# Six of eleven down-projection blocks by seven products in feed-forwards 2 to 4, with part of the weight sums made ahead and kept in DRAM

## The chip, the core and the metric

The kernel runs on one core of a Trainium2 chip. The metric is the device time of one execution in microseconds (us). The engines of the core are TensorE (PE: matmuls; its weight loads are listed as PEld), VectorE (DVE), ScalarE (ACT), GpSimd (POOL) and SyncE (SP), which issues the transfers; 16 DMA engines carry them. MiB is 1,048,576 bytes, GB/s counts in 10^9 bytes.

## The reference

The kernel computes a small streaming encoder in float32: 256 tokens of width 1024, two layers. Each layer is a feed-forward, a mixer, and a second feed-forward, each added to the residual `h`; the mixer is a convolution module in layer 0 and latent attention in layer 1. A normalisation ends the whole. So there are four feed-forwards, which are numbered here 1 to 4 in order of time, with the convolution between 1 and 2 and the attention between 3 and 4.

```python
D_MODEL, SEQ, D_FF = 1024, 256, 2816

def rmsnorm(x, g):
    return x * lax.rsqrt(jnp.mean(x * x, axis=-1, keepdims=True) + 1e-6) * g

def swiglu_ffn(h, w1, w3, w2):
    return (jax.nn.silu(h @ w1) * (h @ w3)) @ w2

for i in range(2):
    h = h + 0.5 * swiglu_ffn(rmsnorm(h, ffn_norm1[i]), ffn1_w1[i], ffn1_w3[i], ffn1_w2[i])
    m = rmsnorm(h, mix_norm[i])
    h = h + (conv_module(m, ...) if i == 0 else mla(m, positions, ...))
    h = h + 0.5 * swiglu_ffn(rmsnorm(h, ffn_norm2[i]), ffn2_w1[i], ffn2_w3[i], ffn2_w2[i])
return rmsnorm(h, final_norm)
```

## The kernel before

**Numbers.** A float32 product is made of three matmuls of a faster format: each operand is split into a high part, which is the operand rounded by a cast, and a low part, which is the rest. `mm3` issues high x low, high x high and low x high into one bank of the accumulator. For weights the split is made in the kernel: ACT casts the raw block (`hi`, L171 and L193), DVE subtracts (`lo`, L175 and L194).

**Weights.** All weights come as blocks of 128 x 2048 float32 (1 MiB). The list `blocks` holds them in order of use. A block is loaded by SP into one of four buffers `raw`, split into one of four pairs `hi`, `lo`, and used. `load` issues one block's load and split; `load_ahead` and `weights` say how far ahead of the matmuls in the code this is written. What a load really waits for is the `raw` buffer of four blocks earlier, which is free when that block's subtraction is done; a subtraction waits for the pair that the matmuls of four blocks earlier read. Subtractions and casts are written `behind` the last urgent instructions of their engine.

**A feed-forward.** It has two stages. The *gate stage* works through 22 weight blocks in six groups (`c` from 0 to 5; the last is half as wide). After a group's matmuls ACT makes the sigmoid-weighted gate, DVE multiplies, and `turn` brings the result into the transposed layout that the next matmuls need: a 32 x 32 transpose on DVE, four DMAs into DRAM (`gd`, L649), and one DMA back (`gb`, L651), all on SP; then ACT and DVE split it into `Gh` and `Gl`. The *down-projection* (class `Rows`, tiles `o`) works through 11 blocks, each of two 128-row slices of w2, for two token tiles of 128 and two column halves of 512: 2 x 2 x 2 = 8 products, 24 matmuls. The last two blocks (9 and 10) are done in `finish`, one output tile after the other, so that the residual additions (L587) and the next stage's normalisation and transposes (`early`, tiles `tp`) can begin with the first tokens.

**Seven products.** A block is a product of two 2 x 2 matrices of tiles (token tiles by row slices, row slices by column halves). For the blocks in `FAST` this is done with seven products instead of eight (21 matmuls), after Strassen and Winograd. It needs four sums of the weight's quarters and sums of the activations. The weight's sums are made by `load_fast` in a second `raw` buffer, `sums`: two by one POOL instruction (L185), one each by two DVE additions (L186, L187). So a fast block takes two `raw` buffers and two pairs, and both `raw` and `sums` are split, 3.5 times 1024 columns in all. The activations' sums are made by `combine` (POOL, L632) from the turned gates. Of the seven products three go straight into output banks and four into banks `p`, which are kept over all fast blocks and combined by `fold` (L572 to L580: ACT, DVE, and POOL, which adds to `h`) behind the last fast block. In every feed-forward `FAST` is (0, 2, 4, 6, 8): fast and plain blocks alternate, and the fold is behind block 8.

**Order.** Each engine works through its instructions in a fixed order. It is set when the kernel is built by a planner that goes through the code's instructions by priority with estimated times; `urgent` raises a function's priority, `order` fixes one instruction's place behind another's on the same engine without a wait. SP issues all loads and the turns' DMAs from one queue.

**The end.** After feed-forward 4 the class `Final` normalises. Its gain row `gf` and its output pieces `hg` have buffers of their own in the feed-forward's pool.

Of the kernel before, what the change touches and what calls it, by code (L numbers as in the profile page):

```python
# [45 lines left out]
FAST = (0, 2, 4, 6, 8)  # L46
# [41 lines left out]
def trunk(ctx: ExitStack, tc: tile.TileContext, x, xt, pos, invf, gains, gfin, wdw,  # L88
# [27 lines left out]
    conv_block = {}  # L116
    for i in range(2):
        for w13, w2 in ((f1w13, f1w2), (f2w13, f2w2)):

            for cc_ in range(5):  # L120
                for m in range(2):
                    blocks += [w13[i, m, 2 * cc_ + a_] for a_ in range(2)]
            blocks += [w13[i, a_, 10] for a_ in range(2)]
            blocks += [("fast", w2[i, a_]) if a_ in FAST else w2[i, a_] for a_ in range(NF // 2)]
# [28 lines left out]
    def load(src, pieces=1):  # L153
        if isinstance(src, tuple) and src[0] == "fast":
            return load_fast(src[1])
        if isinstance(src, tuple):
# [21 lines left out]
    def load_fast(src):  # L178
# [7 lines left out]
        behind(nc.vector.tensor_add(t[:, 2, :], t[:, 0, :], v[:, 3, :]))  # L186
        behind(nc.vector.tensor_add(t[:, 3, :], t[:, 2, :], v[:, 2, :]))  # L187
# [23 lines left out]
    def slots(b):  # L211
        return 2 if isinstance(blocks[b], tuple) and blocks[b][0] == "fast" else 1
# [267 lines left out]
    class Final:  # L480
        def __init__(self, act):
            self.act = act
            self.gf = act.tile([P, D], F32, tag="gf", name="gf")
            nc.sync.dma_start(self.gf, gfin.partition_broadcast(P))

            self.e = [None] * NT
            self.n = [0] * NT
            self.y = {}

        def piece(self, tb, c):  # L490

            n = c.stop - c.start
            t = self.act.tile([P, 512], F32, tag="hg", name=uid("hg"), bufs=4)
# [26 lines left out]
    class Rows:  # L520
        def __init__(self, zh, zl, nk, last=False, sh=None, sl=None):
            self.zh, self.zl, self.nk, self.last = zh, zl, nk, last
            self.sh, self.sl = sh, sl
            self.o = {(tb, d): bank("A", "o") for tb in range(NT) for d in range(2)}
            self.begun = set()
            self.early = max(i for i in range(nk // 2 - 2) if sh is None or i not in FAST)

# [20 lines left out]
        def fast(self, i):  # L548

            n = FAST.index(i)  # L550
# [6 lines left out]
            for o, key, (ah, al), (hi, lo), q in (  # L557
                    (self.p[0], "p1", z(f, 0), raw, 0), (self.o[0, 0], (0, 0), z(f + 1, 0), raw, 2),
                    (self.o[0, 1], (0, 1), s(2), raw, 3), (self.p[2], "p5", z(f, 1), sums, 0),
                    (self.p[3], "q7", s(1), sums, 1), (self.p[1], "q6", s(0), sums, 2),  # L560
                    (self.o[1, 0], (1, 0), z(f + 1, 1), sums, 3)):
                c = slice(q * 512, q * 512 + 512)
                mm3(o, ah, al, hi[:, c], lo[:, c], self.begin(key), isinstance(key, str) and i == FAST[-1])
            if i == FAST[-1]:
                self.fold()
# [46 lines left out]
    def ffn(X, make_next, beside=lambda: None):  # L612
        with tc.tile_pool(name=uid("ffn"), bufs=1) as act:
            return ffn_in(act, X, make_next, beside)

    def ffn_in(act, X, make_next, beside):
        Gh = act.tile([P, NF, S], F32R, tag="Gh", name=uid("Gh"))
        Gl = act.tile([P, NF, S], F32R, tag="Gl", name=uid("Gl"))
        Sh = act.tile([P, 3 * len(FAST), P], F32R, tag="Sh", name=uid("Sh"))
        Sl = act.tile([P, 3 * len(FAST), P], F32R, tag="Sl", name=uid("Sl"))  # L620
# [6 lines left out]
        def combine(i, b0, b1):  # L627

            n = FAST.index(i)
            sx = act.tile([P, 4, P], F32, tag="sx", name=uid("sx"))  # L630
            v = sx.rearrange("p s (i q) -> p s i q", q=32)
            sub = lambda o, a, b: nc.gpsimd.tensor_tensor(o, a, b, op=ALU.subtract)  # L632
            sub(v[:, 3], b1[:, 0], b1[:, 1])
            sub(v[:, 0], b0[:, 0], v[:, 3])
            sub(v[:, 1], b1[:, 0], b0[:, 0])
            sub(v[:, 2], b0[:, 1], v[:, 0])
            split(Sh[:, 3 * n:3 * n + 3, :], Sl[:, 3 * n:3 * n + 3, :], sx[:, :3, :])
            split(Gh[:, 2 * i, tbs(1)], Gl[:, 2 * i, tbs(1)], sx[:, 3, :])

        def turn(c, tb, w, g):  # L640
# [10 lines left out]
            nc.sync.dma_start(b[:, :w], d)  # L651
# [3 lines left out]
            t0 = 0  # L655
            if tb == 1 and 2 * c in FAST:
                t0 = 1
                combine(2 * c, first[c], bv)
            f = slice(4 * c + t0, 4 * c + n)
            gh, gl = (G_[:, f, tbs(tb)].rearrange("p t (i q) -> p t i q", q=32) for G_ in (Gh, Gl))  # L660
            split(gh, gl, bv[:, t0:])
# [49 lines left out]
        o = Rows(Gh, Gl, NF, make_next is Final, Sh, Sl)  # L711
        for i in range(NF // 2 - 2):
            (o.fast if i in FAST else o.block)(i)
# [663 lines left out]
```

## Time and profile before

| | |
|---|---|
| median of three runs | 925.11 us (922.67 to 925.63) |
| profiled execution | 923.62 us, of which span 921.8 us |
| granted TensorE clock | 0.999 |
| PE busy | 909.6 us, 99% of the span |
| DVE, ACT, POOL busy | 74%, 59%, 25% |
| moved by DMA | 191.58 MB, 208 GB/s on average |
| feed-forward 2 in the trace | gates 286 to 404 us, down-projection 404 to 461 us |
| feed-forward 3 in the trace | gates to 583 us, down-projection 583 to 639 us |
| feed-forward 4 in the trace | gates to 858 us, down-projection 858 to 915 us |

A row of the trace in order of time gives the start and the duration in us, the engine, the line of the kernel, the operation, the tile written and the tiles read, the shape, and the number of like instructions that are merged in it; in brackets stands the time for which the engine had been idle, and what ended it. SPq is SP's queue, and its rows are the issue of a transfer, not the transfer. A row of waits gives the waiting engine, tile and line, what it waited for, the total, the count and the longest. A row of a stretch gives its two ends, the length, then the busy time of PE, PEld, DVE, ACT and POOL with the number of instructions, the granted clock, the DMA engines' share and GB/s.

### The profile page before, as it was taken

The numbers are of one execution on the slowest core, as the hardware profiler recorded it, in microseconds if no ns is written. First come the engines' busy times: TensorE is split into PE (matmuls) and PEld (weight loads), VectorE is DVE, ScalarE is ACT, GpSimd is POOL, SyncE is SP. The second block draws the span as 40 slices with busy tenths as digits, with TensorE's granted clock in tenths as the row PEclk, the third lists the DMA queues.
The fourth block names the chain that finished last, engine by engine and source line by source line (L and its number), as shares of the span: only waits on it lengthen the run. The fifth ranks groups of instructions, "written<-read, shape, count | busy, mean of one in ns | idle before, by whom it ended". The sixth has DMA issues, their size and how long they took to land.

```text
span 921.8 us, 12383 instructions
## 1 busy us (share of the span) xinstructions
PE 909.6 (99%) x4293; PEld 755.5 (82%) x4293; DVE 680.9 (74%) x1052; ACT 539.7 (59%) x940; POOL 226.4 (25%) x337
## 2 busy tenths in 40 slices
PE   9999999999999999999999999999999999999997
PEld 6888888898958888888888888888998788888886
DVE  5776877689977666777976667978667476667876
ACT  6964556568877455455474544655666475444643
POOL 1101232379941100232300003224200000013223
PEclk9999999999999999999999999999999999999999
DMA  9976656653307676556756775656441557774651
GB/s 342 350 276 226 203 180 222 240 183 138 138 22 283 244 255 240 189 161 228 299 205 238 252 244 153 228 209 214 183 183 60 186 202 251 246 239 150 219 183 47
DMA packets 60399, 191.58 MB, mean 208 GB/s; under 512 B 11184, under 2 KB 33328, under 8 KB 40752
## 3 DMA queue, kind: packets, MB, share of 16 engines
q1 hardware_dynamic: 59760, 190.09, 58.9%
q8 instruction: 34, 0.56, 0.2%
q10 hardware_dynamic: 576, 0.69, 0.2%
q14 instruction: 29, 0.24, 0.1%
HBM read 178.17 MB, written 12.58 MB: 207 GB/s over the span
## 4 chain that ended last, share of the span: by engine, by line
PE 72%; DVE 8%; DMA 8%; ACT 4%; issue 3%; POOL 3%; SPq 1%; POOLq 0%; ACTq 0%; DVEq 0%
PE u L288 15%; PE u L287 15%; PE u L284 15%; DVE lo L175 5%; PE o L284 3%; PE o L287 3%; PE o L288 3%; PE gate L738 3%; DMA raw<-in_f2w 3%; DMA raw<-in_f1w 3%; PE u L738 3%; POOL sums L185 3%; PE o L978 2%; ACT hi L171 1%; DVE lo L194 1%
## 5 line engine op out<-in xcount | busy, mean ns | idle before, releaser
L175 DVE TENSOR_TENSOR lo<-raw,hi 128x1024 fp32r<-128x1024 f32 (+1 forms) x246 | 296.3, 1240 | 74.4 <-ACT hi L171 74.1
L171 ACT CAST hi<-raw 128x1024 fp32r<-128x1024 f32 (+1 forms) x250 | 247.9, 1046 | 147.7 <-PE u L288 107.9
L288 PE MATMUL u<-hi,Xl 128*128 128x512 f32 x688 | 267.8, 390 | 0.7 <-DVE Xl L345 0.7
L284 PE MATMUL u<-lo,Xh 128*128 128x512 f32 x688 | 268.1, 390 | 0.1
L287 PE MATMUL u<-hi,Xh 128*128 128x512 f32 x688 | 267.7, 389 | 0.0
L288 PEld LDWEIGHTS u<-hi,Xl 128*128 128x128 f32 x688 | 129.1, 188 | 28.2 <-DVE Xl L345 1.6
L284 PEld LDWEIGHTS u<-lo,Xh 128*128 128x128 f32 x688 | 129.2, 188 | 27.3 <-DVE lo L175 0.5
L287 PEld LDWEIGHTS u<-hi,Xh 128*128 128x128 f32 x688 | 129.2, 188 | 26.6
L185 POOL TENSOR_TENSOR sums<-raw 128x1024 f32<-128x1024 f32 x20 | 54.2, 2710 | 162.4 <-DMA raw<-in_f2w 52.7
L284 PE MATMUL o<-lo,Gh 128*128 128x512 f32 (+1 forms) x236 | 91.5, 388 | 0.7 <-DVE lo L175 0.7
L287 PE MATMUL o<-hi,Gh 128*128 128x512 f32 (+1 forms) x236 | 91.0, 386 | 0.0
L288 PE MATMUL o<-hi,Gl 128*128 128x512 f32 (+1 forms) x236 | 91.0, 386 | 0.0
L632 POOL TENSOR_TENSOR sx<-gb 128x128 f32<-128x128 f32 x20 | 10.2, 509 | 316.7 <-DMA gb<-gd 316.7
L624 ACT CAST Gh<-gb 128x512 fp32r<-128x512 f32 (+2 forms) x48 | 25.8, 539 | 63.6 <-DMA gb<-gd 63.5
L193 ACT CAST hi<-sums 128x1024 fp32r<-128x1024 f32 x40 | 41.2, 1052 | 30.7 <-PE u L288 14.7
L786 DVE SCALAR_TENSOR_TENSOR acc<-V,dw,acc 128x128 f32<-128x128 f32 (+1 forms) x174 | 57.8, 411 | 0.0
L625 DVE TENSOR_TENSOR Gl<-gb,Gh 128x512 fp32r<-128x512 f32 (+2 forms) x48 | 33.2, 705 | 31.2 <-ACT Gh L624 31.1
L194 DVE TENSOR_TENSOR lo<-sums,hi 128x1024 fp32r<-128x1024 f32 x40 | 56.1, 1432 | 0.0
L284 PEld LDWEIGHTS o<-lo,Gh 128*128 128x128 f32 x236 | 44.3, 188 | 11.0 <-DVE lo L175 2.3
L288 PEld LDWEIGHTS o<-hi,Gl 128*128 128x128 f32 x236 | 44.3, 188 | 8.9
L287 PEld LDWEIGHTS o<-hi,Gh 128*128 128x128 f32 x236 | 44.3, 188 | 8.8
L814 ACT ACTIVATE prod<-V,dw 128x128 f32<-128x128 f32 (+1 forms) x129 | 48.0, 418 | 2.8 <-POOL Y L815 1.4
(247 smaller groups left out, 1325.7 us busy)
## 6 DMA issues: line engine op xcount, KB each, us to landing
raw<-in_f2w SPq DMA_DIRECT2D x66, 1024.0 KB, 4.8
raw<-in_f1w SPq DMA_DIRECT2D x64, 1024.0 KB, 5.0
raw<-in_cw SPq DMA_DIRECT2D x12, 1024.0 KB, 5.2
gd<-gt SPq DMA_DIRECT2D x160, 64.0 KB, 2.7
gb<-gd SPq DMA_DIRECT2D x40, 256.0 KB, 3.4
raw<-in_wo SPq DMA_DIRECT2D x4, 1024.0 KB, 4.8
raw<-in_wuq SPq DMA_DIRECT2D x3, 1024.0 KB, 4.8
raw<-in_f1w SPq DMA_DIRECT2D x8, 256.0 KB, 6.2
```

Of the source, the lines that this page charges most:

```text
L171: behind(nc.scalar.copy(hi[:, c], raw[:, c]))
L175: behind(nc.vector.tensor_sub(lo[:, c], raw[:, c], hi[:, c].bitcast(F32)))
L185: behind(nc.gpsimd.tensor_tensor(t[:, 0:2, :], v[:, 0:4:3, :], v[:, 1:2, :].to_broadcast([P, 2, 512]), op=ALU.add))
L193: behind(nc.scalar.copy(hi[:, c0:c1], x[:, c0:c1]))
L194: behind(nc.vector.tensor_sub(lo[:, c0:c1], x[:, c0:c1], hi[:, c0:c1].bitcast(F32)))
L284: mm = nc.tensor.matmul(o, ah, bl, start=start, stop=False)
L287: nc.tensor.matmul(o, ah, bh, start=False, stop=False)
L288: return nc.tensor.matmul(o, al, bh, start=False, stop=stop)
L625: nc.vector.tensor_sub(dl, x, dh.bitcast(F32))
L738: mm = nc.tensor.matmul(u[:, t], w[:, c], X.x[:, k, t], start=(k == 0), stop=(k == KT - 1))
L786: ins = nc.vector.scalar_tensor_tensor(out if j == j1 - 1 else y, v, w, y, op0=ALU.mult, op1=ALU.add)
L814: prod = nc.scalar.activation(p, v, AF.Copy, scale=w)
```

## The change

In feed-forward 1 the fast blocks remain 0, 2, 4, 6 and 8. In feed-forwards 2 to 4 they are 0, 2, 4, 5, 6 and 7. Blocks 0 and 2 make their sums as before. The sums of blocks 4 to 7 are made during the gate stage of the same feed-forward by `sum_ahead`: the block is loaded into a `raw` buffer (a *job*, behind the loads of the gate blocks 4, 7, 10 and 13), DVE makes the four sums in place by four additions, and SP stores them to DRAM. Later `load_summed` loads three quarters of the raw block and all four sums, as two and one transfers, behind the last turn in SP's order.

```diff
-FAST = (0, 2, 4, 6, 8)
+FAST = ((0, 2, 4, 6, 8), (0, 2, 4, 5, 6, 7))
+AHEAD = {4: 4, 5: 7, 6: 10, 7: 13}
...
+            first = len(blocks) == 22
+            for a_ in range(NF // 2):
+                w = w2[i, a_]
+                if not first and a_ in AHEAD:
+                    jobs[len(blocks) - a_ - 22 + AHEAD[a_]] = (a_, w)
+                    w = ("summed", w, a_)
+                elif a_ in FAST[0 if first else 1]:
+                    w = ("fast", w)
+                blocks.append(w)
...
-        behind(nc.vector.tensor_add(t[:, 2, :], t[:, 0, :], v[:, 3, :]))
-        behind(nc.vector.tensor_add(t[:, 3, :], t[:, 2, :], v[:, 2, :]))
+        behind(nc.vector.tensor_add(t[:, 3, :], t[:, 0, :], v[:, 3, :]))
+        behind(nc.vector.tensor_add(t[:, 2, :], t[:, 3, :], v[:, 2, :]))
+        return split_fast(raw, sums)
+
+    def sum_ahead(a, src):
+        raw = rawp.tile([P, HB], F32, tag="raw", name=uid("job"))
+        nc.sync.dma_start(raw, src)
+        v = raw.rearrange("p (b n) -> p b n", n=512)
+        for to, x, y in ((0, 0, 1), (1, 1, 3), (3, 0, 3), (2, 3, 2)):
+            behind(nc.vector.tensor_add(v[:, to, :], v[:, x, :], v[:, y, :]))
+        summed[a] = dram.tile([P, HB], F32, tag=f"summed{a}", name=uid("summed"))
+        nc.sync.dma_start(summed[a], raw)
+
+    def load_summed(src, a):
+        raw = rawp.tile([P, HB], F32, tag="raw", name=uid("raw"))
+        sums = rawp.tile([P, HB], F32, tag="raw", name=uid("sums"))
+        for c in (slice(0, 512), slice(1024, HB)):
+            order(nc.sync.dma_start(raw[:, c], src[:, c]), last_turned[-1].ins)
+        order(nc.sync.dma_start(sums, summed[a]), last_turned[-1].ins)
+        return split_fast(raw, sums)
...
     def load_to(last):
         while len(loaded) < last:
-            loaded.append(load(blocks[len(loaded)], PIECES))
+            b = len(loaded)
+            loaded.append(load(blocks[b], PIECES))
+            if b in jobs:
+                sum_ahead(*jobs[b])
```

`split_fast` is the loop of casts and subtractions that stood at the end of `load_fast`. `last_turned` collects each turn's DMA back from DRAM.

With two fast blocks in one gate group (4 and 5, 6 and 7), `combine` makes both blocks' activation sums by the same four POOL instructions at twice the width, and the splits are wider too. The fold stands behind block 7, the last fast one; block 8 is plain. In `Final`, `gf` uses the buffer of the low part of the normalised activations, `Xl`, and the pieces use the turn's buffers:

```diff
-            self.gf = act.tile([P, D], F32, tag="gf", name="gf")
+            self.gf = xp.tile([P, KT, S], F32, tag="Xl", name="gf").rearrange("p k t -> p (k t)")[:, :D]
...
-            t = self.act.tile([P, 512], F32, tag="hg", name=uid("hg"), bufs=4)
+            tag, bufs = (("gb", 3), ("gt", 2))[len(self.y.get(tb, ())) % 2]
+            t = self.act.tile([P, 512], F32, tag=tag, name=uid("hg"), bufs=bufs)
...
             b = act.tile([P, 512], F32, tag="gb", name=uid("gb"), bufs=3)
-            nc.sync.dma_start(b[:, :w], d)
+            last_turned.append(nc.sync.dma_start(b[:, :w], d))
...
-            if tb == 1 and 2 * c in FAST:
-                t0 = 1
-                combine(2 * c, first[c], bv)
+            if tb == 1 and 2 * c in fasts:
+                count = 2 if 2 * c + 1 in fasts else 1
+                own = slice(1, n, count)
+                combine(c, count, first[c], bv)
```

In feed-forward 4 the output tile of the second tokens and the right columns, into which only plain blocks are accumulated, is added to `h` after block 8 instead of after block 7.

More of the change, by code (lines that the diff above doesn't have):

```diff
@@ L116, in trunk @@
     conv_block = {}
+    jobs = {}
     for i in range(2):
@@ L211, in slots @@
     def slots(b):
-        return 2 if isinstance(blocks[b], tuple) and blocks[b][0] == "fast" else 1
+        return 2 if isinstance(blocks[b], tuple) and blocks[b][0] in ("fast", "summed") else 1
     def load_ahead(ahead=W_BUFS - 2):
@@ L710, in ffn_in @@
                 turn(c, tb, w, g)
-        o = Rows(Gh, Gl, NF, make_next is Final, Sh, Sl)
+        o = Rows(Gh, Gl, NF, make_next is Final, Sh, Sl, fasts)
         for i in range(NF // 2 - 2):
-            (o.fast if i in FAST else o.block)(i)
+            (o.fast if i in fasts else o.block)(i)
             beside()
```

59 lines of the change are left out of this document (32 added, 27 removed).

## The prediction

> **What bounds the kernel now.** I read the page first, for the engine that is busy throughout, then the waits of TensorE, then its order of time in one feed-forward.
>
> ```profile
> PE 909.6 (99%) x4293; PEld 755.5 (82%) x4293; DVE 680.9 (74%) x1052; ACT 539.7 (59%) x940; POOL 226.4 (25%) x337
> ...
> PE 72%; DVE 8%; DMA 8%; ACT 4%; issue 3%; POOL 3%; SPq 1%; POOLq 0%; ACTq 0%; DVEq 0%
> ```
>
> TensorE (PE) is busy 99% of 921.8 us. Its waits:
>
> ```profile
> PE u L288 <- DVE Xl L345: 0.7, 2, 0.4
> PE o L284 <- DVE lo L175: 0.7, 2, 0.4
> ...
> PE a L288 <- DVE Xl L345: 0.3, 1, 0.3
> ```
>
> All that TensorE waits in the change's neighbourhood is there (total, times, longest). So time falls only with matmuls that go or with these small waits, and rises only where the change makes TensorE wait. The price of a matmul, from feed-forward 2 (the first matmul of down-projection blocks 0 and 8):
>
> ```profile
> 404.13 0.39 PE L284 MATMUL p<-lo,Gh 128*128 128x512 f32 x1
> ...
> 444.93 0.39 PE L284 MATMUL p<-lo,Gh 128*128 128x512 f32 x1
> ```
>
> Between them lie blocks 0 to 7, four of seven products (7 x 3 = 21 matmuls) and four plain (2 x 2 x 2 x 3 = 24): 180 matmuls in 40.80 us, 0.2267 us each, without a gap. (0.39 is one matmul's own time; they overlap.) A plain block is 5.44 us, a fast one 4.76.
>
> **The change part by part.**
>
> *Products.* Six fast blocks in place of five in feed-forwards 2, 3 and 4: 3 x 3 = 9 matmuls less, 9 x 0.2267 = **-2.04 us**. Nothing hides matmuls on a gapless TensorE, so this much is certain.
>
> *The sums of blocks 4 to 7.* Before, a fast block's sums were made just ahead of its use: one POOL instruction and two DVE adds, which stand in DVE's fixed order before other blocks' subtractions. In feed-forward 4 this cost TensorE something:
>
> ```profile
> 888.23 2.40 POOL L185 TENSOR_TENSOR sums<-raw 128x1024 f32<-128x1024 f32 x1 [8.13 <-DMA raw<-in_f2w]
> 890.67 0.69 DVE L186 TENSOR_TENSOR sums<-sums,raw 128x512 f32<-128x512 f32 x1 [4.09 <-POOL sums L185]
> 893.01 1.22 DVE L175 TENSOR_TENSOR lo<-raw,hi 128x1024 fp32r<-128x1024 f32 x1
> 893.66 0.39 PE L288 MATMUL o<-hi,Gl 128*128 128x512 f32 x1
> 894.28 0.50 PE L284 MATMUL o<-lo,Gh 128*128 128x512 f32 x1 [0.23 <-DVE lo L175]
> 894.62 0.40 PE L287 MATMUL o<-hi,Gh 128*128 128x512 f32 x1
> ```
>
> DVE sat 4.09 us behind POOL with block 8's sums, so block 7's second subtraction ended at 894.23. From 893.66 to 894.62 are 0.96 us where two matmuls take 0.45. Sums now remain only for blocks 0 and 2, long before block 7: **-0.5 us**. Late next there is the cast of a plain block, which waits for a weight slot and not for sums.
>
> *The jobs beside the gates.* Four a feed-forward: 1 MiB read, four DVE adds in place, 1 MiB written. The adds are like the 0.69 above, 0.6 apart: 16 x 0.6 = 9.6 us of DVE.
>
> ```profile
> 286.00:404.10 118.10, 118.10 (x522) 97.78 (x521) 83.39 (x97) 61.04 (x81) 16.61 (x20) 1.00 0.65 222
> 448.00:452.00 4.00, 4.00 (x20) 3.30 (x19) 3.41 (x4) 3.43 (x4) 1.73 (x1) 1.00 1.01 428
> ...
> 365.06 0.33 SPq L168 DMA_DIRECT2D raw<-in_f2w  x1
> ```
>
> The first row is the gate stage (busy us of PE, PEld, DVE, ACT, POOL, then clock, DMA share, GB/s): DVE goes from 83.4 to 93 of 118 us. With the DMA engines full they move 428 GB/s (next row), that is 2.5 us a MiB, so 8 MiB is 20 us and the share goes from 0.65 to about 0.82. Both fit. What waits: the store stands in SP's queue until its adds are done, and behind it stand the next gate loads and the turns' small DMAs. The last row says what those loads can bear: it is the last gate block's load, issued at 365.06 for matmuls that begin one block (5.44) before 404.13, at 398.7, so 33 us ahead. A job holds one of four raw buffers for a time, which takes at most one block, 5.4 us, of that lead. DVE queues subtractions behind adds that wait for their load; a weight slot comes free three blocks (16 us) before its next use, and a subtraction pair is 2.3. I take 0. Without that cover the adds would cost 9.6 us a feed-forward (upper bound); below nothing I see no reason for.
>
> A 1 MiB store does not occur in the trace. From below it is the load's 2.5 us, from above the 4.8 of a whole load from issue to landing; it ends some 60 us before it is read, so either is free.
>
> *The run of blocks 4 to 7.* Each needs 0.75 MiB of raw columns and 1 MiB of sums: 1.75 x 2.5 = 4.4 us of DMA, 3.5 subtractions and casts of 1024 columns.
>
> ```profile
> 430.43 2.35 DVE L194 TENSOR_TENSOR lo<-sums,hi 128x1024 fp32r<-128x1024 f32 x2
> 429.76 2.00 ACT L171 CAST hi<-raw 128x1024 fp32r<-128x1024 f32 x2
> 412.41 0.34 SPq L651 DMA_DIRECT2D gb<-gd  x1
> raw<-in_f2w SPq DMA_DIRECT2D x66, 1024.0 KB, 4.8
> ```
>
> DVE needs 3.5 x 1.17 = 4.1 us, ACT 3.5, TensorE 4.76: TensorE stays the slowest, DMA close behind. The new order puts these loads behind the last turn, which was issued at 412.41, 8.3 us into the stage. I follow feed-forward 2 (block starts from 404.13: block 4 at 424.5, then 429.3, 434.0, 438.8, block 8 at 443.6), four raw buffers and four weight slots used in turn. Block 4's raw half is issued about 412.7 and lands within 4.8, 417.5; its sums land 2.5 later, 420.0; block 5's halves follow by 424, and block 4 has both subtractions done by 422.5, its start being 424.5. From there each half's subtraction waits for the slot of the half two blocks earlier: block 6's sums get theirs at 429.3, are done by 431.6, needed at 436.1 (after three products); block 7's: 434.0, 436.3, 440.9. **4.5 us are left at each**, and its load is issued at 426.8 and lands about 431.7, 2.3 before the slot. I take 0. The other end stands below as a rival.
>
> The Trainium skill, "DMA: Bandwidth & Descriptors", section "Where 436 GB/s comes from", sets the HBM limit of a core at about 358 GB/s; the row above, with 428, contradicts it here. By that limit a block's 1.84 MB would take 5.1 us (an estimate by that page), 0.4 more than TensorE, 1.5 over the four; it speaks against the change, and is why the supply rival gets more than a token chance.
>
> *Sums of activations for two blocks at once, the swapped order of two sums, the final norm's buffers.* POOL subtracts 256 columns instead of 128 twice, due over 20 us later; same instructions in another order; the gain row is now loaded into a buffer whose last reader is the gate matmul at 858, against a first use at 909. One DVE add of the last stage comes a block later. Zero each; without cover some 0.7 us (one DVE instruction).
>
> *The fold behind block 7.* Its four POOL and five other instructions now start about 440.9 instead of 447.04 (2.1 us after the last fast block's start, as before), while the finishing groups start at 449.0, not 449.7.
>
> ```profile
> 447.04 0.57 ACT L572 COPY fold<-p 128x512 f32<-128x512 f32 x1
> 457.78 0.68 DVE L579 TENSOR_TENSOR fold<-p,fold 128x512 f32<-128x512 f32 x1
> 458.38 1.87 DVE L587 TENSOR_TENSOR h<-o,h 128x512 f32<-128x512 f32 x3
> 458.60 1.29 POOL L580 TENSOR_TENSOR h<-h,fold 128x512 f32<-128x512 f32 x1 [1.83 <-DVE fold L579]
> 460.57 1.47 PE L327 MATMUL tp<-ident,h 128*128 128x128 f32 x12
> 462.11 0.40 PE L287 MATMUL u<-hi,Xh 128*128 128x512 f32 x1
> 462.79 0.50 PE L288 MATMUL u<-hi,Xl 128*128 128x512 f32 x1 [0.28 <-DVE Xl L345]
> 639.08 1.47 PE L327 MATMUL tp<-ident,h 128*128 128x128 f32 x12
> ...
> 641.29 0.50 PE L288 MATMUL a<-hi,Xl 128*128 128x512 f32 x1 [0.28 <-DVE Xl L345]
> 183.38 1.95 PE L453 MATMUL tp<-dR,h 128*128 128x128 f32 x16
> 185.08 0.47 PE L284 MATMUL o<-lo,Gh 128*128 128x512 f32 x1
> ```
>
> Before, the fold ran into the next stage's subtractions; three additions to h came in one lump at 458.38, so all twelve transposes stand behind the last product (460.57), and the next matmuls wait for casts and subtractions: from 462.11 to 462.79 0.45 us too much, with its neighbours about 0.6. The joint at 639.08 is its twin. In feed-forward 1, where the additions were not late, transposes stand inside the stream (183.38, products again at 185.08). Now the fold, 12.9 us long in feed-forward 2 (447.04 to 459.89), ends at 453.8 at worst, while the second group ends at 449.0 + 5.44 = 454.4. So the first rows' eight transposes can go in among the last two groups and those waits go: 2 x 0.6 less some 0.1 for the change of shape: **-1.1 us**, between 0 (the planner leaves them behind) and -1.3. I take -1.1, as feed-forward 1 shows it. Feed-forward 4 ends in no such joint.
>
> **The sum.** -2.04 - 0.5 - 1.1 = -3.6 us. The profiled execution took 923.62 (span 921.8 and 1.8 around it), so 920.0 by its own time; it lies 1.5 below the median of the three runs, 925.11 (they spread over 3.0 us). Against the median: 921.5, a ratio of 0.996. About 0.3%, 2.8 us, is what a measurement of this kernel can tell from no change, so the forecast stands just beyond it.
>
> **The rivals.**
>
> *A, the forecast*, 921.5 (920.0 to 923.0): chance 0.50.
>
> *B, the joints stay as they are*: the planner fixes each engine's order when the kernel is built and may leave the transposes behind the last product. For it: the twins do so now. Against: the additions' lateness goes. -2.04 - 0.5: 922.6. Chance 0.25.
>
> *C, DVE stands at a job's add for a load that is late*, as it did for 4.09 us above, and subtractions behind it come late. One such stand cost TensorE 0.5 there; beside the gates the slots are 16 us ahead, which speaks against. With 12 jobs, at 0.3 each: +3.6, so 925.1. Chance 0.13.
>
> *S, the run starves, and it is slower.* Place: blocks 4 to 7, loads behind the last turn, 7 MiB (7.34 MB) in 19.0 us of products. They have 19.0 + 2.3 + 4.5 = 25.8 us before TensorE waits: nothing is lost down to 284 GB/s. Slower by 2.8 than before needs (2.8 + 3.6) / 3 = 2.1 us a feed-forward, so 263 GB/s or less. The mean of this stage before was:
>
> ```profile
> 404.10:461.00 56.90, 56.90 (x254) 47.11 (x253) 48.23 (x52) 32.63 (x42) 17.93 (x13) 1.00 0.69 244
> ```
>
> At 244 the run takes 30.1, 4.3 too long, 12.9 over three: 925.1 - 3.6 + 12.9 = 934.4. For it: that mean, and SP issues in order, so one blocked issue holds all behind it. Against: 244 was all that was asked, and 428 came when more was. Chance 0.12.
>
> **How the numbers follow.** Faster by over 0.3%: 0.85 of A and 0.3 of B, 0.50. Slower: S and a little of C, 0.14. The rest, 0.36, within. The range 919.5 to 927.0 holds A, B and C with the runs' spread, and leaves out most of S and a little below.
>
> **What would show it.** Right: four fast blocks in a row at 4.76 us each with no wait for a subtraction; no wait at block 7 of feed-forward 4; no POOL sums beyond blocks 0 and 2; transposes inside the last products of feed-forwards 2 and 3, and the 0.45 us gone. Wrong: waits for DVE subtractions in blocks 5 to 8 (S, with loads landing after their slot is free), waits in the gates (C), or twelve transposes still behind the last product (B).

## The result, and the profile after

The changed kernel took **930.72 us** (median of six runs, 929.86 to 933.54) against 924.8 for the kernel before (six runs as well): a ratio of **1.0075**, 95% interval 1.0057 to 1.0093. It is slower; the prediction, 921.5 in a range of 919.5 to 927.0, had the wrong sign. Its profiled execution took 929.86 us with a span of 928.1, 6.25 more than before.

The engines' line of the page and the waits of TensorE (waiting engine, tile and line, what it waited for; total, times, longest) show where it went:

```profile
PE 909.0 (98%) x4284; PEld 753.3 (81%) x4284; DVE 706.3 (76%) x1082; ACT 544.8 (59%) x940; POOL 210.6 (23%) x316
```

```profile
PE p L326 <- DVE lo L233: 2.6, 3, 1.2
PE tp L369 <- DVE h L630: 2.3, 2, 1.2
PE o L326 <- DVE lo L189: 1.7, 3, 1.2
```

TensorE has the nine matmuls less that were forecast (4293 to 4284), and 6.6 us of waits in these three rows, where the three rows quoted of before have 1.7 together. By stretches, from a down-projection's first product to the next stage's first matmul (the last one to the end of the span):

| stretch | before | after | difference |
|---|---|---|---|
| down-projection of feed-forward 2 | 57.67 | 60.44 | +2.77 |
| of feed-forward 3 | 57.67 | 61.21 | +3.54 |
| of feed-forward 4, with the end | 63.98 | 66.06 | +2.08 |
| up to feed-forward 2's down-projection | 404.13 | 403.02 | -1.10 |
| between the down-projections | 120.83 and 217.55 | 120.30 and 217.04 | -0.53 and -0.51 |

Everything that was lost was lost in the three down-projections, each of which has 0.68 us of products less. There are four places. Each size below is the excess of the step between two neighbouring matmuls over the usual 0.227.

*In the run of blocks 4 to 7:* 3.05 us, at 435.37 (0.39), 617.79 (1.39) and 900.03 (1.27). The trace in order of time, in feed-forward 3, for block 6's sums:

```profile
607.13 0.33 SPq L223 DMA_DIRECT2D sums<-summed  x1
615.43 1.99 ACT L232 CAST hi<-sums 128x1024 fp32r<-128x1024 f32 x2 [3.15 <-DMA sums<-summed]
616.51 2.36 DVE L233 TENSOR_TENSOR lo<-sums,hi 128x1024 fp32r<-128x1024 f32 x2 [2.52 <-ACT hi L232]
617.79 0.50 PE L326 MATMUL p<-lo,Gh 128*128 128x512 f32 x1 [1.23 <-DVE lo L233]
```

The transfer was issued at 607.13 and landed at 615.33, 8.2 us later. ACT and DVE stand idle for it (3.15 and 2.52), and TensorE for the subtraction: the data are late, no engine is.

*Behind the run:* 2.20 us at 452.49, 634.01 and 911.52, where `finish` waits for a subtraction of blocks 9 and 10.

*At the joints:* 2.64 us. The trace at feed-forward 2's end:

```profile
454.61 4.58 DVE L189 TENSOR_TENSOR lo<-raw,hi 128x1024 fp32r<-128x1024 f32 x3
459.12 1.87 DVE L630 TENSOR_TENSOR h<-o,h 128x512 f32<-128x512 f32 x3
459.85 0.65 PE L369 MATMUL tp<-ident,h 128*128 128x128 f32 x4 [1.17 <-DVE h L630]
461.51 0.60 PE L369 MATMUL tp<-ident,h 128*128 128x128 f32 x4
463.11 0.60 PE L369 MATMUL tp<-ident,h 128*128 128x128 f32 x4
```

The transposes did move in among the last products, four at a time, as forecast. But the first of them waits for the additions to `h`, which stand in DVE's order behind the subtractions of the next stage's first two blocks.

*At the end:* from the last matmul's start (919.85; before 914.89) to the end of the span 8.22 us, before 6.94.

```profile
910.33 2.28 POOL L621 TENSOR_TENSOR h<-h,fold 128x512 f32<-128x512 f32 x1
912.58 1.30 POOL L623 TENSOR_TENSOR h<-h,fold 128x512 f32<-128x512 f32 x1
913.90 1.29 DVE L630 TENSOR_TENSOR h<-o,h 128x512 f32<-128x512 f32 x2 [1.84 <-POOL h L623]
```

Before, the same first addition waited for TensorE:

```profile
908.26 0.69 DVE L587 TENSOR_TENSOR h<-o,h 128x512 f32<-128x512 f32 x1 [2.08 <-PE o L288]
```

The fold is stretched out between subtractions, POOL's part of it ends at 913.88, and DVE's closing chain starts 5.95 us ahead of the last matmul instead of 6.63.

With 0.51 at 588.35, where the third down-projection waits for the last gate, these waits make 9.68 us; the products (-2.04), the wait of before at 894.28 (-0.51), the old joint waits (-1.04) and the earlier part (-1.10) take off 4.7. That leaves 5.0 of the 6.25; of the other 1.3, 0.8 is the matmul right behind seven of these waits, which each time starts another 0.11 us late, and the rest lies in smaller pieces, which I did not trace.

The page's list of transfers (KB each, median us from issue to landing) shows the change in the latencies; before they were 4.8 for `raw<-in_f2w`, 3.4 for `gb<-gd` and 2.7 for `gd<-gt`:

```profile
raw<-in_f2w SPq DMA_DIRECT2D x58, 1024.0 KB, 7.5
summed<-job SPq DMA_DIRECT2D x12, 1024.0 KB, 8.1
sums<-summed SPq DMA_DIRECT2D x12, 1024.0 KB, 7.6
gd<-gt SPq DMA_DIRECT2D x160, 64.0 KB, 3.9
gb<-gd SPq DMA_DIRECT2D x40, 256.0 KB, 6.2
```

The gate stage of feed-forward 2 took no longer (118.10, as before), with the jobs in it:

```profile
284.90:403.00 118.10, 118.10 (x522) 97.78 (x521) 91.51 (x110) 60.62 (x80) 19.64 (x20) 1.00 0.79 286
```

### The profile page after: what moved, and what is told of

The parts are those of the page before. It is cut to its first block, busy times and chain, and to the rows that moved or that the text cites. A ratio compares the mean times of both kernels' runs of the same rounds, so it can differ in the third digit from the quotient of the medians.

```text
span 928.1 us, 12462 instructions
## 1 busy us (share of the span) xinstructions
PE 909.0 (98%) x4284; PEld 753.3 (81%) x4284; DVE 706.3 (76%) x1082; ACT 544.8 (59%) x940; POOL 210.6 (23%) x316
## 4 chain that ended last, share of the span: by engine, by line
PE 60%; DMA 16%; DVE 11%; ACT 6%; issue 4%; POOL 2%; SPq 1%; POOLq 0%; ACTq 0%; DVEq 0%
PE u L330 12%; PE u L326 12%; PE u L329 12%; DMA gb<-gd 5%; DMA sums<-summed 5%; DVE lo L189 4%; PE gate L783 3%; PE o L326 3%; PE o L329 3%; PE o L330 3%; DMA raw<-in_f2w 3%; PE u L783 3%; DVE lo L233 3%; ACT hi L185 2%; DMA gd<-gt 2%
## 5 line engine op out<-in xcount | busy, mean ns | idle before, releaser
L185 ACT CAST hi<-raw 128x1024 fp32r<-128x1024 f32 (+1 forms) x244 | 241.9, 1046 | 123.7 <-PE u L330 62.1
L675 POOL TENSOR_TENSOR sx<-gb 128x128 f32<-128x128 f32 (+1 forms) x17 | 12.1, 714 | 333.0 <-DMA gb<-gd 172.4
L326 PE MATMUL o<-lo,Gh 128*128 128x512 f32 (+1 forms) x218 | 84.1, 388 | 2.1 <-DVE lo L189 1.7
L330 PE MATMUL o<-hi,Gl 128*128 128x512 f32 (+1 forms) x218 | 84.2, 386 | 0.0
L329 PE MATMUL o<-hi,Gh 128*128 128x512 f32 (+1 forms) x218 | 84.2, 386 | 0.0
L232 ACT CAST hi<-sums 128x1024 fp32r<-128x1024 f32 x46 | 46.2, 1049 | 29.8 <-DMA sums<-summed 19.5
L233 DVE TENSOR_TENSOR lo<-raw,hi 128x512 fp32r<-128x512 f32 (+1 forms) x46 | 45.7, 1019 | 9.8 <-ACT hi L232 9.8
L326 PEld LDWEIGHTS o<-lo,Gh 128*128 128x128 f32 x218 | 40.9, 188 | 11.9 <-DVE lo L189 3.0
L330 PEld LDWEIGHTS o<-hi,Gl 128*128 128x128 f32 x218 | 41.0, 188 | 8.1
L329 PEld LDWEIGHTS o<-hi,Gh 128*128 128x128 f32 x218 | 41.0, 188 | 8.0
```

The costliest lines, as they stand in the source:

```text
L185: behind(nc.scalar.copy(hi[:, c], raw[:, c]))
L232: behind(nc.scalar.copy(hi[:, c0:c1], x[:, c0:c1]))
L233: behind(nc.vector.tensor_sub(lo[:, c0:c1], x[:, c0:c1], hi[:, c0:c1].bitcast(F32)))
L326: mm = nc.tensor.matmul(o, ah, bl, start=start, stop=False)
L329: nc.tensor.matmul(o, ah, bh, start=False, stop=False)
L330: return nc.tensor.matmul(o, al, bh, start=False, stop=stop)
```

## The experiments

All ratios are to the kernel before, run on the same chip. A trace is of one execution of a kernel. For half_sums and run_late it was the fastest one (921.48 and 922.26 us), 4.7 and 3.0 us below the median, so what their other executions waited for is not known.

### One: how much is loaded, and where the fold stands

The first three runs ask whether the waits come from the run's transfers or from the fold's new place.

**half_sums** loads half of each block of stored sums, and the splits of the other half read the same columns again:

```diff
-        order(nc.sync.dma_start(sums, summed[a]), last_turned[-1].ins)
+        order(nc.sync.dma_start(sums[:, :1024], summed[a][:, :1024]), last_turned[-1].ins)
```

> The changed kernel, but of the four stored sums of blocks 4 to 7 only the first 1024 columns are loaded, and the splits of the other half read these columns again: casts, subtractions and matmuls are the same in number and size, the run's transfers are 1.25 MiB a block instead of 1.75. It leaves out half of the stored sums, so its output is not the reference's. Theory 'supply' (loads that take 7 to 8 us each in a full DMA, with four raw buffers, make the run's subtractions late, and everything behind them late too): the waits for L233 in the run go (3.0 us over three feed-forwards), and with them the waits for block 10's subtraction (2.2) and for the additions to h at the joints (2.6), so about 923 us or less. Theory 'fold' (the fold behind block 7 stands in DVE's order ahead of block 10's second subtraction and slows it, whatever the loads do): only the 3.0 us go, 927 to 928 us.

Measured: 926.2 (921.5 to 929.5), ratio 1.0018 [1.0000, 1.0036]. In the trace, that of the fastest execution, no wait in the run is left, none behind it, and one at a joint (0.94). The median lies between the two forecasts. So the run's transfers are part of the cause; how large a part is open.

**fold_late** calls the fold behind block 8 again:

```diff
-            if i == self.fasts[-1]:
-                self.fold()
...
+            if i == 8:
+                o.fold()
```

> The changed kernel with the fold called behind plain block 8 instead of behind fast block 7; loads, jobs and fast blocks as they are. Theory 'fold': the waits for block 10's subtraction and at the joints go (up to 4.9 us), the run's 3.0 us stay: about 926 us. Theory 'supply': the run's waits stay and the late subtractions stay late: 929 us or more.

Measured: 931.94, ratio 1.0091 [1.0062, 1.0119]. The waits of all three kinds stay.

**fold7_only** has five fast blocks, 0, 2, 4, 6 and 7, no jobs, and the fold behind block 7:

```diff
-FAST = ((0, 2, 4, 6, 8), (0, 2, 4, 5, 6, 7))
-AHEAD = {4: 4, 5: 7, 6: 10, 7: 13}
+FAST = ((0, 2, 4, 6, 8), (0, 2, 4, 6, 7))
+AHEAD = {}
```

> No jobs and no DRAM sums; in feed-forwards 2 to 4 the fast blocks are 0, 2, 4, 6 and 7 with sums made on chip as before: five fast blocks as in the kernel before, the last one moved from 8 to 7 and with it the fold. Theory 'fold': slower than before by the 4.9 us of block 10 and the joints, 928 to 930 us. Theory 'supply': no full DMA, so as before within 1.5 us, 923 to 926 us.

Measured: 922.73 (921.6 to 925.1), ratio 0.9987 [0.9976, 0.9998]. Its transposes wait for nothing, and the matmuls behind the joint follow without the gap that stood there before:

```profile
461.94 0.60 PE L369 MATMUL tp<-ident,h 128*128 128x128 f32 x4
462.30 0.48 PE L326 MATMUL u<-lo,Xh 128*128 128x512 f32 x1
462.61 0.39 PE L329 MATMUL u<-hi,Xh 128*128 128x512 f32 x1
462.84 0.40 PE L330 MATMUL u<-hi,Xl 128*128 128x512 f32 x1
```

1.2 us less (0.2 to 2.2 by the interval). The joint waits of before are gone, as the prediction's step on the fold said; so is the wait at block 7 of feed-forward 4, which stood at 894.28 before. The fold's place isn't what made the changed kernel slow.

### Two: where the sums are made

**no_jobs** (`AHEAD = {}`: the same six blocks, every sum made on the chip), **spread7** (blocks 0, 1, 2, 4, 6 and 7, no jobs) and **mixed** (jobs for blocks 5 and 7 only).

> The changed kernel's six fast blocks (0, 2, 4, 5, 6, 7) and its fold behind block 7, with all sums made on chip: no jobs, 1 MiB a block. The four blocks in a row now cost DVE two adds more each, 5.2 us a block against TensorE's 4.76. Theory 'supply': the loads are no limit, DVE falls behind by up to 2 us a feed-forward: 922 to 928 us, below the changed kernel's 930.7. Theory 'fold': the joints' and block 10's waits are there as in the changed kernel, and DVE is later still: 930 us or more.

> Six fast blocks without any job: 0, 1, 2, 4, 6 and 7, sums on chip, fold behind block 7; there are pairs, but no four in a row late in the stage. Blocks 0 to 2 are loaded and split while the gates still run. Theory 'supply' (and DVE's 5.2 us a block only hurting in a long run): the 9 matmuls less (2.0 us) and the joints' gain (the fold behind 7 alone gave 1.2) add up, 920 to 922 us. If three fast blocks at the start starve as well: 925 us or more.

> Jobs for blocks 5 and 7 alone; blocks 4 and 6 make their sums on chip. Six fast blocks, fold behind block 7, output complete. The run's transfers are 5.5 MiB instead of 7, DVE gets 4.1 and 5.2 us of work in turn against TensorE's 4.76. Theory 'supply': most of the waits of the run go and those behind it with them, 922 to 925 us. If DVE's order around the on-chip sums is the limit, as in the kernel without jobs, 928 us or more.

Measured: 936.16, 934.84 and 936.56; ratios 1.0128, 1.0114 and 1.0128, all with intervals above 1.008. The waits of no_jobs:

```profile
PE p L326 <- DVE lo L233: 5.8, 6, 1.2
PE tp L369 <- DVE h L630: 2.8, 2, 1.4
PE o L326 <- DVE lo L233: 1.5, 2, 0.9
```

All three lie above what theory 'supply' allowed (928, 922 and 925). Six fast blocks with their sums made on the chip are slower than with jobs, in both places that were tried. But mixed, which stores half of the sums, is no faster than no_jobs, so the time doesn't simply follow the number of sums made on the chip; what in DVE's order costs it was not traced.

### Three: the jobs alone, the run alone

**jobs_only** makes and stores the sums but never reads them (fast blocks 0, 2, 4, 6 and 8). **run_only** has no jobs; in place of the stored sums it loads the block itself, the same bytes for the same instructions:

```diff
-        order(nc.sync.dma_start(sums, summed[a]), last_turned[-1].ins)
+        order(nc.sync.dma_start(sums, src), last_turned[-1].ins)
...
-            if b in jobs:
-                sum_ahead(*jobs[b])
```

> The twelve jobs alone (1 MiB read, four adds, 1 MiB written beside the gates), with the down-projections as before the change: fast blocks 0, 2, 4, 6, 8 with sums on chip, the stored sums are never read, the fold behind block 8. If the jobs are hidden beside the gates, as the trace of the changed kernel says (its gate stages take as long as before): 923 to 925 us. If they are what makes the half-sums kernel's runs lie between 921 and 929 us: 925 to 928 us, with runs as far apart.

> The run alone, without the jobs: blocks 4 to 7 load 0.75 MiB of raw columns and, in place of the stored sums, the 1 MiB raw block itself. It leaves the weight sums of blocks 4 to 7 out, so its output is not the reference's; transfers, casts, subtractions, matmuls and the fold in the run are those of the changed kernel. Theory 'supply': the waits for L233, block 10 and the joints are all there, 929 to 932 us as the changed kernel. If the jobs or the read of what was just stored cost something of their own, it is nearer 925 us.

Measured: jobs_only 924.4, ratio 1.0000 [0.9985, 1.0015]; run_only **922.09**, ratio 0.9977 [0.9960, 0.9994]. In run_only TensorE doesn't wait in the run at all. Neither half makes the kernel slower; both together cost 8.6 us more than the run alone. But run_only is not without waits: in its trace there are 0.55 us behind the run (451.29) and 1.27 and 0.72 at the joints (458.62 and 636.74), so those two places wait without a late run too. The bytes alone aren't the reason for the waits in the run, as three stretches of 26 us from the run's first loads on show (PE, PEld, DVE, ACT, POOL, clock, DMA share, GB/s); the changed kernel first, then run_only:

```profile
413.00:439.00 26.00, 25.77 (x114) 21.03 (x113) 17.39 (x18) 15.16 (x19) 0.00 (x0) 1.00 0.94 338
596.00:622.00 26.00, 24.77 (x109) 20.19 (x108) 17.97 (x18) 15.53 (x18) 0.00 (x0) 1.00 0.95 350
873.00:899.00 26.00, 25.92 (x115) 21.11 (x113) 17.15 (x18) 15.17 (x19) 0.00 (x0) 1.00 0.93 339
```

```profile
411.00:437.00 26.00, 26.00 (x117) 21.52 (x116) 17.09 (x18) 13.39 (x17) 0.00 (x0) 1.00 0.92 328
591.00:617.00 26.00, 26.00 (x117) 21.52 (x116) 18.53 (x19) 14.70 (x18) 0.00 (x0) 1.00 0.97 348
866.00:892.00 26.00, 26.00 (x116) 21.55 (x115) 17.69 (x20) 14.69 (x18) 0.00 (x0) 1.00 0.94 346
```

The rate is the same within 10 GB/s. The last two loads of sums in each run took 6.1 to 7.7 us to land in run_only and 6.4 to 8.2 in the changed kernel. What differs is the beginning. Feed-forward 3 in the changed kernel, SP's queue (`gd<-gt` is a turn's way into DRAM, `gb<-gd` its way back; L182 loads a gate block, L222 the run's first columns):

```profile
551.15 6.83 SPq L694 DMA_DIRECT2D gd<-gt  x8
562.44 0.35 SPq L182 DMA_DIRECT2D raw<-in_f1w  x1
562.90 0.88 SPq L696 DMA_DIRECT2D gb<-gd  x2
...
595.58 0.34 SPq L696 DMA_DIRECT2D gb<-gd  x1
595.96 0.43 SPq L222 DMA_DIRECT2D raw<-in_f1w  x1
```

and in run_only:

```profile
549.57 3.94 SPq L692 DMA_DIRECT2D gd<-gt  x8
554.12 1.27 SPq L694 DMA_DIRECT2D gb<-gd  x2
560.46 0.33 SPq L182 DMA_DIRECT2D raw<-in_f1w  x1
...
590.19 0.34 SPq L694 DMA_DIRECT2D gb<-gd  x1
590.87 0.35 SPq L222 DMA_DIRECT2D raw<-in_f1w  x1
```

Down-projection 3 begins at 583.76 and at 582.52. So the run's first load is issued 12.2 us behind the start in one and 8.3 in the other. With the jobs a gate load that waits for its `raw` buffer until 562.44 stands ahead of both of a turn's `gb` transfers, the turns fall behind, and the run's loads stand behind the last turn. The jobs alone don't do all of that: jobs_only issued its last `gb` transfer 8.1, 8.4 and 10.8 us behind the start of down-projections 2, 3 and 4, where it was 8.3, 7.5 and 8.4 before the change, 9.5, 11.8 and 10.8 in the changed kernel, and 8.2, 8.6 and 11.3 in fold7_only, which has no jobs. How the delay is handed on from turn to turn was not followed. This became theory L (late start). Its rival R was that reading the stored sums is slow.

### Four: late start, or slow sums

**jobs_run_src** is the changed kernel with the run_only line for the loads, so that the instructions of every engine are the same in the same order. **early_jobs** has `AHEAD = {4: 1, 5: 4, 6: 7, 7: 10}`. **run_late** and, later, **run_later** are run_only with two and three small stores ahead of the run's loads:

```diff
+        if a == 4:
+            d = dram.tile([32, P], F32, tag="late", name=uid("late"))
+            for i in range(2):
+                e = nc.sync.dma_start(d, last_gt[0][:32, :P])
+                order(e, last_turned[-1].ins)
+                last_turned.append(e)
```

**no_order** drops the three order edges of `load_summed`:

```diff
-            order(nc.sync.dma_start(raw[:, c], src[:, c]), last_turned[-1].ins)
-        order(nc.sync.dma_start(sums, summed[a]), last_turned[-1].ins)
+            nc.sync.dma_start(raw[:, c], src[:, c])
+        nc.sync.dma_start(sums, summed[a])
```

> The changed kernel with the jobs as they are, but blocks 4 to 7 load their second megabyte from the input instead of the stored sums (the sums that are multiplied are wrong, bytes and instructions on every engine are those of the changed kernel, in the same order). Theory L (late start: the jobs make the last turns late, the run's loads stand behind the last turn and are issued 10 to 12 us after the down-projection's start instead of 8, which uses up what is left before TensorE waits): as slow as the changed kernel, 929 to 932, with TensorE waiting for subtractions in the run. Rival R (reading the stored sums is slower than reading an input): 922 to 923, no waits in the run.

> The changed kernel with its jobs at gate blocks 1, 4, 7 and 10 instead of 4, 7, 10 and 13, some 16 us earlier. Theory L: the turns have caught up by the end of the gates, the run's loads are issued about 8 us after the start of the down-projection again, and most of the waits go: 922 to 925. Rival R: the stored sums are still read, so 929 to 932.

> The run alone (no jobs, the second megabyte from the input, 922.1 before), with two small stores of 16 KB put between the last turn and the run's loads on SP's queue, the second waiting for the first, so that the loads start some 2.3 us later. The output is not the reference's, as before. Theory L: TensorE waits in the run as in the changed kernel, 924 to 928. Rival R, or if the start doesn't matter: 921.5 to 923.

> The changed kernel without the order edges that put the run's loads behind the last turn: block 4's raw columns then stand ahead of the last turn's transfers in SP's queue, its sums between them. Theory L: the loads start 2 to 4 us earlier, the 3.05 us of waits in the run go, and part of the 2.2 behind it: 924 to 927. Rival R: 929 to 932.

> The run alone, no jobs, with three small stores one behind the other ahead of its loads, some 4 us instead of 2.3; the output is not the reference's, as in the run alone. Theory L: the loads are then issued 11.5 to 13 us after the start of the down-projection, later than in the changed kernel (9.9 to 12.2), and TensorE waits in each of the three runs, 0.4 to 2.6 us each: 927 to 932. If the start alone doesn't make the waits: 925 or less.

Measured:

| kernel | median | ratio, interval | first load behind the stage's start, feed-forwards 2, 3, 4 | TensorE's waits in the run |
|---|---|---|---|---|
| run_only | 922.09 | 0.9977 [0.9960, 0.9994] | 7.8, 8.3, 8.8 | 0, 0, 0 |
| run_late | 925.3 | 1.0014 [1.0002, 1.0026] | 9.8, 10.2, 11.9 | 0, 0, 0.8 |
| run_later | 927.51 | 1.0054 [1.0027, 1.0080] | 12.2, 12.2, 12.4 | 1.5, 1.2, 0.9 |
| early_jobs | 929.32 | 1.0059 [1.0032, 1.0086] | 8.8, 10.4, 9.3 | 0, 0.7, 0 |
| changed kernel | 930.72 | 1.0075 [1.0057, 1.0093] | 9.9, 12.2, 11.2 | 0.4, 1.4, 1.3 |
| jobs_run_src | 931.87 | 1.0089 [1.0071, 1.0107] | 10.2, 13.1, 11.3 | 0, 2.7, 1.7 |
| no_order | 926.62 | 1.0038 [1.0027, 1.0050] | 2.6, 4.0, 2.7 (block 4's raw columns; its sums 10.5, 10.9, 10.8) | 0, 0, 0 |

R falls: with the sums read from the input the kernel is as slow. And jobs_run_src and run_only differ in the jobs alone, so with this order of blocks it is the jobs that make the start late. L holds for the run: with no jobs at all, three small stores (3.55 us of SP's queue) make the waits. run_later:

```profile
592.90 3.55 SPq L225 DMA_DIRECT2D late<-gt  x3
596.49 0.90 SPq L229 DMA_DIRECT2D raw<-in_f1w  x2
```

```profile
PE p L331 <- DVE lo L240: 2.6, 5, 0.7
```

Of the ten starts up to 10.4 us in the table two have a wait in the run; of the eight behind that, all. The start isn't everything: fold_late waited 1.3 us in feed-forward 2 with a start at 9.6, and half_sums, with 1.25 MiB a block instead of 1.75, did not wait in the run with starts at 8.8, 12.1 and 11.6. So it takes the late start and the bytes together. An earlier start of block 4's raw columns (no_order) takes the waits in the run and behind it away.

Two things missed. early_jobs came out 4 us above its expectation, where R would have had it: its starts are only partly back, and its first job's additions now stand ahead of and between the additions to `h` at the joints:

```profile
458.79 0.68 DVE L214 TENSOR_TENSOR job<-job 128x512 f32<-128x512 f32 x1
459.40 0.68 DVE L630 TENSOR_TENSOR h<-o,h 128x512 f32<-128x512 f32 x1
460.00 0.67 DVE L214 TENSOR_TENSOR job<-job 128x512 f32<-128x512 f32 x1
460.60 0.68 DVE L630 TENSOR_TENSOR h<-o,h 128x512 f32<-128x512 f32 x1
```

And no_order's joints got worse:

```profile
PE tp L369 <- DVE h L630: 4.0, 2, 2.4
```

So the joint has a cause of its own, as run_only's joints show too.

### Five: the joint

**joint** loads and splits the next stage's second block behind the first addition to `h`; **no_order_joint** has that and no order edges.

```diff
-            parts = weights(2)
+            joint = self.fasts == FAST[1] and not self.last
+            parts = weights(2, True, 1 if joint else W_BUFS - 2)
...
                     urgent(add)(tb, c, o)
+                    if joint and i == 0:
+                        load_ahead()
```

> The changed kernel, but the second weight block of the next stage is loaded and split behind the first of the four additions to h in feed-forwards 2 and 3, where it stood ahead of it in DVE's order. Theory J (the transposes at the two joints wait because DVE has two blocks' subtractions ahead of the additions, 2.4 us each): the two waits of 1.3 us go, 2.6 less, 927 to 929; the waits in the run stay. Rival K (DVE is late at the joint only because the run was late, and the order of the additions doesn't matter): 930 to 932.

> The same edit in the kernel whose run loads don't stand behind the last turn (926.6, with 4.3 us of waits at its two joints and none in the run). Theory J: the 4.3 us of joint waits go for the most part, 922 to 924. Rival K: there the run wasn't late, so the joint waits have another cause and stay, 926 to 927.5.

Measured: joint 929.44, ratio 1.0084 [1.0055, 1.0114]; no_order_joint 924.27, ratio 1.0011 [0.9995, 1.0027]. In joint no transpose waits for `h` any more; 0.6 at each joint is back as the wait for `Xl`, as before the change. In no_order_joint 0.43 of 4.3 us is left, and the time falls by 2.4, to just above its forecast. In both traces the waits for `h` go with the order, so theory J holds: it is the place of the additions behind the two blocks' subtractions. The time of joint doesn't show it; it missed its 927 to 929, and its interval overlaps that of the changed kernel. Its trace has a costlier place elsewhere, its run, whose loads start at 11.4, 12.2 and 11.8, with 1.5 and 1.3 us of waits in feed-forwards 2 and 4; in feed-forward 3, where TensorE itself had stood 0.87 us for a gate earlier, there is none.

### Six: the last feed-forward

**six_six_five** is no_order_joint with five fast blocks (0, 2, 4, 6 and 7) and no jobs in feed-forward 4:

```diff
+FAST = ((0, 2, 4, 6, 8), (0, 2, 4, 5, 6, 7), (0, 2, 4, 6, 7))
...
-                if not first and a_ in AHEAD:
+                if kind == 1 and a_ in AHEAD:
```

> Feed-forwards 2 and 3 as in the kernel before this one (six fast blocks with jobs, loads not behind the last turn, the second weight block split behind the first addition); feed-forward 4 with five fast blocks, 0, 2, 4, 6 and 7, all sums on the chip, no jobs, the fold behind block 7. The kernel before this one reached feed-forward 4's down-projection 1.7 us ahead of the original and lost 2.4 after it, 1.0 of it to a late turn and about 2 in the tail; five fast blocks with the fold behind block 7 took 63.6 us from there to the end, the original 64.0. If the loss is the jobs' and the sixth block's in the last feed-forward: 856.1 + 63.6 + 1.8, 921.5, 920 to 923. If the tail is late for another reason: 923.5 to 925.

Measured: 924.25 (922.2 to 926.1), ratio 1.0005 [0.9996, 1.0014]. The tail went back from 8.98 us to 7.16, so the longer tail belongs to the sixth block or its jobs in the last feed-forward. run_only has the sixth block there without the jobs and a tail of 7.24, so it is not the block by itself; how the jobs lengthen the tail was not traced. The time didn't follow, and lies where it was expected if the tail had another reason: 64.5 us from the start of the last down-projection instead of the 63.6 hoped for, with a wait of 0.74 at 885.53, and the start itself came at 858.95, not 856.11. Of all that was run, run_only apart (its output is another), fold7_only is the only one whose interval lies below the kernel before, by 0.1%.

## Why the prediction was wrong

*Products:* right, nine matmuls less.

*The sums of blocks 4 to 7:* the wait at 894.28 is gone, as forecast. Waits of the same kind, 2.20 us, came at blocks 9 and 10. They are gone in no_order, but run_later has a late run and none of them, and run_only a punctual run and one of 0.55: that the late run makes them is not shown.

*The jobs beside the gates, at zero:* right for what it counted. TensorE's gate stage is 118.10 us as before, DVE is at 91.5 us in it (93 forecast), the DMA share at 0.79 (0.82), and jobs_only measured 1.0000. It was incomplete: the step named the turns' small DMAs behind a waiting store, and then asked only what the gate loads can bear. The run's loads hang on the last turn, and so they began 9.9, 12.2 and 11.2 us behind their stage's start, where the next step counted on 8.6.

***The run of blocks 4 to 7, at zero, is the step that failed***, in two of its terms. The first is the start: "issued about 412.7" was 8.6 us behind the stage's start, behind the last turn of a kernel without jobs; with them it was 9.9, 12.2 and 11.2. The second is the landing: "lands within 4.8" took the median of a kernel whose DMA engines were 0.69 busy in this stage. In feed-forward 2 block 6's sums took from 424.90 to 432.91 and block 7's from 429.98 to 437.33, 8.0 and 7.4 us. "4.5 us are left at each" was therefore about 1.5, an estimate from the starts above: waits begin some 10 us behind the stage's start, and 8.6 was counted on. Neither term alone made TensorE wait. run_only has the slow landings and starts at 7.8 to 8.8, and its run costs nothing; and a start that is 1.3 to 3.6 us later would have fitted into 4.5. Together they cost 3.05 us in the run.

*The fold behind block 7, at -1.1:* right alone (fold7_only, -1.2, with the wait at 894.28 gone as well). In the changed kernel the old joint waits went (-0.53 and -0.51 in the following stages) and a new one of 1.3 each took their place. I had asked when the fold ends and not what stands in DVE's order between the fold and the additions: two blocks' subtractions, on an engine that worked without a break from 444.77 to the end of the first addition, 459.8. run_only's joints, with a run on time, wait 1.99 us, so this part of the forecast would have failed without the late run too.

*Wider combine, swapped sums, Final's buffers, at zero:* the end grew by 1.28 us. run_only has all three edits and an end of 7.24, 0.30 more than before, so they are at most a small part of it; the rest goes with the jobs of feed-forward 4 (six_six_five). The fold's place is not the reason: fold_late has 8.08.

*The rivals:* S had the right place and sign and the wrong mechanism. It was to decide at 263 GB/s or less; the run moved 338 to 350 and still waited, since its loads were issued later and took longer to land, while the rate was no lower. C (DVE standing at a job's add) did not occur on TensorE's path, and B's twelve transposes behind the last product did not either.

The Trainium skill, "DMA: Bandwidth & Descriptors", section "Where 436 GB/s comes from", gives about 358 GB/s as what the HBM side allows a core. The run's means, 338 to 350 GB/s with the engines 0.93 to 0.95 busy, lie just below it. Single slices of the changed kernel's page (23.2 us each) lie above it, at 378 and 385, as do the 428 over 4 us that the prediction shows, so it isn't a hard bound here; that the run's means come near it doesn't show that it is what limits them:

```profile
GB/s 341 338 298 219 216 167 219 227 183 154 120 74 255 335 378 373 172 155 359 325 189 339 365 385 137 197 357 241 182 181 74 154 209 361 373 341 139 227 345 46
```

## What to carry to other kernels

Price a transfer by its latency under the load that the change itself makes, not by the median of the kernel before: here 1 MiB of sums took 6.4 to 8.2 us instead of 4.8 once four buffers were refilled back to back, and up to 10.7 where six loads were issued together. When loads are ordered behind a small transfer, follow the chain that ends in that transfer too; and when two parts of a change each "cost nothing", ask whether they draw on the same margin, and run each alone and both together. At a joint, read the engine's order between the last thing that frees it and the thing that is waited for.

## What was not expected of the hardware

A VectorE subtraction of 128 x 1024 took 1.22 us alone, and 1.72 and 2.00 while POOL worked at the fold's additions, one of which (910.33, shown above) took 2.28 instead of 1.30 us:

```profile
905.22 2.04 POOL L616 TENSOR_TENSOR h<-h,fold 128x512 f32<-128x512 f32 x1 [50.24 <-ACT fold L615]
906.62 1.72 DVE L189 TENSOR_TENSOR lo<-raw,hi 128x1024 fp32r<-128x1024 f32 x1
909.09 1.29 POOL L619 TENSOR_TENSOR h<-h,fold 128x512 f32<-128x512 f32 x1 [1.83 <-DVE fold L618]
909.47 2.00 DVE L189 TENSOR_TENSOR lo<-raw,hi 128x1024 fp32r<-128x1024 f32 x1
```

In these rows the two nearly took turns: each became longer by most of the time for which the other was still at work. The subtraction at 906.62 began 0.64 us before POOL's addition ended and took 0.50 longer; that at 909.47 began 0.91 before and took 0.78 longer; POOL's addition at 910.33 began 1.14 before that subtraction ended and took 0.98 longer. The same happens at the joint of feed-forward 2: four subtractions from 452.96 on took 6.24 us there, where two took 2.36 with POOL idle (616.51, above). So the fold's additions on POOL may be a second reason why DVE came late to `h`; no run takes it out.
